# Up pieces of a tile side by side, the second piece's low products first, and down steps in groups of one or two

## The chip, the cores and the metric

The kernel runs on one core of a Trainium2 chip. The metric is the device time of one execution in microseconds (us); lower is better. Times of before are three runs: a median of 1104.94 us, from 1104.69 to 1105.36.

Five engines take part, each with its own in-order list of instructions: TensorE (PE: matrix products; PEld is its loading of the stationary operand), VectorE (DVE), ScalarE (ACT), GpSimd (POOL) and SyncE (SP). In this kernel SP and POOL issue the transfers. Engines wait for each other by semaphores.

## The reference

One layer of a transformer on 256 tokens of width 2048, in float32: two groups of eight attention heads, an output projection, and a feed-forward network (FFN) with a short causal convolution. The change is about the FFN's products, and about a helper that the second attention group uses too.

```python
def conv_ffn(h, w_up_l, conv_w_l, conv_b_l, w_down_l):
    u = h @ w_up_l                                  # (256 x 2048) @ (2048 x 11264)
    c = u.shape[-1]
    u = lax.conv_general_dilated(u, conv_w_l[:, None, :], ..., padding=[(2, 0)],
                                 feature_group_count=c) + conv_b_l
    gate, val = jnp.split(u, 2, axis=-1)
    return (jax.nn.silu(gate) * val) @ w_down_l     # (256 x 5632) @ (5632 x 2048)
```

## The kernel before

**Splits.** Products run in a rounded float32 type. To keep precision every operand is split in a high half (rounded) and a low half (the rest), and a product is made of three: high times high, high times low, low times high. For a weight tile of 128 x 2048 values (1 MB) `load` (L201) brings the raw values, ScalarE casts the high half (L208, `w_hi`) and VectorE subtracts the low half (L209, `w_lo`).

**Up pieces.** `from_features` (L250) makes a piece: 8 slices of 128 rows of the weight against the features `hT`, for two blocks of 128 output columns. The 16 high products (L257) have 512 columns, since `hT` holds its high and low halves side by side; the 16 low products (L264) have 256, with the high half of `hT` alone. In before, the high products of a piece always come first. Two pieces (kh = 0 and 1) add up to a tile of 256 features in PSUM, in one bank pair `pu`; tiles come in twos, one for the gate and one for the value. The first tile of the FFN (c0 = 0) does this in two halves of 4 slices. `feature_major` uses the same helper in the second attention group (8 tiles).

**Down steps.** The down product of a part of the FFN is done for two halves of the columns (c = 0 and 1024), each in seven products instead of eight (a scheme of Strassen's kind, with sums of activations prepared in `val_follows` and sums of weights in `down_in_seven`). Each product is a step: `in_three` (L230) with 8 high and 4 low products of 512 columns. In the order of before:

1. the split activations (pairs) of the first token half with `w11` (bank_a), loads `w11`
2. the sum T5 with `w` = `w11` + `w12` (bank_b), loads `w12`; `first_sum` (L999, VectorE) makes `w`; after the split POOL issues two accumulating transfers (L969): `w22` into `w` and `w22` into `w12`
3. pairs with `w21` (bank_c), loads `w21`
4. S2 with `w` (bank_a), then `w21` is accumulated into `w`
5. T7 with `w12` (bank_a), the third sum of weights
6. S4 with `w22` (bank_b), loads `w22`
7. pairs with `w` (bank_a)

After a step VectorE adds its bank to the output rows (`added`, L946).

**What follows an up tile.** ScalarE copies half of the tile (L847), VectorE adds it (L848, `t`) and scales (L850, `up`); ScalarE forms the three taps (L857, L864), VectorE adds them (L869); then Silu for a gate tile, or, for a value tile, the product (L884), its split (L887, L889) and, in the second half of a part, four combinations (L901 to L904). When a part's last value tile is done, its sums are cast (L911, four on ScalarE) and subtracted (L916, four on VectorE).

**The order.** The FFN's 44 blocks of 128 gate columns (and the 44 of the values) are cut into six parts, five of 8 blocks and a last one of 4; a tile is two blocks. `ORDER` and `LAST_ORDER` write out which step follows which: `u` is an up piece, `s` a down step of the part before, a digit a plain down piece of the last part. A loop over the steps records all instructions under a manual schedule, so each engine's list has their order: at step n the load of step n+6, what follows earlier tiles (`follow`, twice in each step), the split of step n+2, the first sum of step n+4, and then the products of step n. The buffers: 4 raw tiles (`wraw2`), 3 high and 3 low (`whi2`, `wlo2`); in attention there are 3, 2 and 2. A buffer is given back when its last reader is done, so a high half of step n+2 waits for the high products of step n-1.

Of the kernel before, what the change touches and what calls it, by code (L numbers as in the profile page):

```python
# [14 lines left out]
P = 128  # L15
D = 2048
S = 256
NT = S // P
KT = D // P
# [5 lines left out]
NFT = DFF // P  # L25
# [12 lines left out]
FFN_PARTS = [(f, min(f + 8, NFT)) for f in range(0, NFT, 8)]  # L38


ORDER = "uuusususususususususususususus"
LAST_ORDER = "uususususususussss0s1ss3s2"


@with_exitstack
def hybrid_layer(
# [19 lines left out]
    nc = tc.nc  # L66
# [65 lines left out]
    hT = big.tile([P, KT, 2, S], F32R, name="hT")  # L132
# [86 lines left out]
    def rows_of(w, k0, n, c0, cols):  # L219
        return w[k0 * P : (k0 + n) * P, c0 : c0 + cols].rearrange("(k p) c -> p k c", p=P)  # L220
# [17 lines left out]
    def token_major(lhs, w, k0, nk, c0, cols):  # L238

        acc = psa.tile([P, NT, 512], F32, name="acc", tag="acc")  # L240
        for k in range(0, nk, 4):
            parts = weights(rows_of(w, k0 + k, 4, c0, cols), 4, cols)
            in_three(
                [acc[:, t, :cols] for t in range(NT)], parts, 4,
                lambda i, part, t: of_half(lhs(k + i), part, t), k == 0, k + 4 == nk,
            )
            step()
        return acc

    def from_features(acc, parts, kh, n=8):  # L250

        hi, lo = parts
        for i0 in range(0, 8, n):
            for i in range(i0, i0 + n):
                k = 8 * kh + i
                for j in range(2):
                    nc.tensor.matmul(  # L257
                        acc[:, j, :], hi[:, i, j * P : (j + 1) * P],
                        hT[:, k].rearrange("p a b -> p (a b)"), start=k == 0, stop=False,
                    )  # L260
            for i in range(i0, i0 + n):
                k = 8 * kh + i
                for j in range(2):
                    nc.tensor.matmul(  # L264
                        acc[:, j, S:], lo[:, i, j * P : (j + 1) * P], hT[:, k, 0, :],
                        start=False, stop=k == KT - 1,
                    )

    def feature_major(w, c0, pool, tag):

# [14 lines left out]
    with ExitStack() as actx:  # L285
# [9 lines left out]
        def project(c0, cols):  # L295
            return token_major(lambda k: hT[:, k], wi, 0, KT, c0, cols)
# [198 lines left out]
        low = big.tile([P, 2, 16 * P], F32R, name="low", tag="x2")  # L495
# [41 lines left out]
        for j in range(3):  # L537
            acc = project(2 * WF + 344 * j, 344)
            n = 344 if j < 2 else 336
# [211 lines left out]
        for half in range(2):  # L751
# [6 lines left out]
            acc = project(B0 + 2 * WF + 512 * half, 512)  # L758
# [16 lines left out]
        for group in range(2):  # L775
# [3 lines left out]
            for c in range(4):  # L779
                acc = token_major(lambda k: oT[group * NH + k], wo, group * NH, NH, 512 * c, 512)  # L780
# [6 lines left out]
                if c == 0:  # L787
                    pg = psb.tile([P, NT], F32, name="pg", tag="t")
                    for t in range(NT):
                        nc.tensor.matmul(  # L790
                            pg[:, t : t + 1], ssq[group][:, t * P : (t + 1) * P], ones[:, 0:1],
                            start=t == 0, stop=t == NT - 1,
# [86 lines left out]
    T5, S2, S4, T7 = (0, 1), (1, 1), (1, 0), (0, 0)  # L879
# [71 lines left out]
    def down_in_seven(part, c0):  # L951


        nk = (part.f_hi - part.f_lo) // 2
        w11, w12, w21, w22 = (
            rows_of(wd, part.f_lo + nk * h, nk, c0 + i * 512, 512) for h in range(2) for i in range(2)
        )
        mem = {}

        def of_pairs(h, t):  # L960
            return lambda i, p, _: part.pairs[(nk * h + i) // 2][:, p, i % 2, t * P : (t + 1) * P]

        def of_sums(q):
            n, t = q
            return lambda i, p, _: part.sums[i // 2][:, p, n, i % 2, t * P : (t + 1) * P]

        def plus(into, src):

            nc.gpsimd.dma_start(  # L969
                mem[into][:, : nk * 512].rearrange("p (a b) -> p a b", a=nk), src, accum_op=ALU.add  # L970
            )

        def product(bank, new, lhs, weights, to, op=ALU.add, load_=None, sums=None, then=None):
            t, h = to

            def loads():
                for name, src in load_ or ():
                    mem[name] = load(src)

            def prepare():  # L980
                mem["parts", bank, to] = split(mem[weights], nk, 512)
                if then:
                    then()

            def matmuls():
                if new:
                    pool, tag = (psf, "a") if bank == "bank_a" else (psb, "t")
                    mem[bank] = pool.tile([P, 512], F32, name=bank, tag=tag)
                in_three([mem[bank]], mem["parts", bank, to], nk, lhs(), new, True, more=not new)

            new_step(
                loads, sums, prepare, matmuls,
                lambda: added(c0 + 512 * h, mem[bank], t, op),
            )

        def first_sum():
            mem["w"] = wsum.tile([P, 2048], F32, name="w_sum", tag="w_sum")
            w, x, y = (mem[m][:, : nk * 512] for m in ("w", "11", "12"))
            dve.tensor_tensor(w, x, y, op=ALU.add)  # L999

        product("bank_a", True, lambda: of_pairs(0, 0), "11", (0, 0), load_=[("11", w11)])
        yield
        product(
            "bank_b", True, lambda: of_sums(T5), "w", (1, 1), load_=[("12", w12)],
            sums=first_sum, then=lambda: (plus("w", w22), plus("12", w22)),
        )
        yield
        product("bank_c", True, lambda: of_pairs(1, 0), "21", (0, 0), load_=[("21", w21)])
        yield
        product("bank_a", False, lambda: of_sums(S2), "w", (0, 1), ALU.subtract, then=lambda: plus("w", w21))  # L1010
        yield
        product("bank_a", False, lambda: of_sums(T7), "12", (1, 1), ALU.subtract)
        yield
        product("bank_b", False, lambda: of_sums(S4), "22", (0, 1), load_=[("22", w22)])
        yield
        product("bank_a", False, lambda: of_pairs(1, 1), "w", (1, 0))
        yield

    def down_plain(part, c):

        n = (part.f_hi - part.f_lo) // 4

        ends = LAST_ORDER[-1] == str(c // 512)
        sizes = [(0, 0, 512), (1, 0, 256), (1, 256, 256)] if ends else [(t, 0, 512) for t in range(NT)]
# [41 lines left out]
            piece(kh)  # L1066
            yield

    last = None
    for f_lo, f_hi in FFN_PARTS:  # L1070
        part = Part(f_lo, f_hi)
        steps_of = {

            "u": [
                p for f in range(f_lo, f_hi, 2) for follows in (gate_follows, val_follows)
                for p in [up_pieces(part, f, follows)] * 2
            ],
            "s": [g for c in (0, 1024) for g in [down_in_seven(last, c)] * 7 if last],
        }
        if f_hi == NFT:  # L1080
            steps_of |= {str(i): [down_plain(part, 512 * i)] for i in range(4)}
        for g in ORDER if f_hi < NFT else LAST_ORDER:
            if steps_of[g]:
                next(steps_of[g].pop(0))
        assert not any(steps_of.values())
        last = part

    ctx.enter_context(
# [76 lines left out]
```

## Time and profile before

| | before |
|---|---|
| median of three runs | 1104.94 us |
| profiled execution | 1104.87 us |
| its span, first to last instruction | 1103.1 us |
| instructions in it | 14847 |
| L257, high products of up pieces | 1664 |
| L264, low products of up pieces | 1664 |
| splits into halves (L208, L209) | 226 each |
| transfers from HBM | 242.89 MB |

The profile is of one execution, on the hardware. Busy times of PE are modelled and products overlap in the pipeline, so its cadence is read from the starts of successive products in the timeline, not from their lengths. A group in the timeline has its start, its length, the engine, the line, the operation, the tiles, the shapes and how often it comes; in brackets stands how long the engine was idle before it and what ended that. In the table of stretches ("windows") each row has the stretch, then the busy time of PE, PEld, DVE, ACT and POOL with their counts, the granted clock of TensorE as a share of full speed, the busy share of the DMA engines and the GB/s. In the list of waits a row has who waited for whom, the sum in us, how often, and the longest.

### The profile page before, as it was taken

The numbers are of one execution on the slowest core, as the hardware profiler recorded it, in microseconds if no ns is written. First come the engines' busy times: TensorE is split into PE (matmuls) and PEld (weight loads), VectorE is DVE, ScalarE is ACT, GpSimd is POOL, SyncE is SP. The second block draws the span as 40 slices with busy tenths as digits, with TensorE's granted clock in tenths as the row PEclk, the third lists the DMA queues.
The fourth block names the chain that finished last, engine by engine and source line by source line (L and its number), as shares of the span: only waits on it lengthen the run. The fifth ranks groups of instructions, "written<-read, shape, count | busy, mean of one in ns | idle before, by whom it ended". The sixth has DMA issues, their size and how long they took to land. (4 is left out here: it accounts for less than half of the span.)

```text
span 1103.1 us, 14847 instructions
## 1 busy us (share of the span) xinstructions
PE 1097.9 (100%) x5872; PEld 951.4 (86%) x5872; DVE 876.2 (79%) x940; ACT 701.6 (64%) x879; POOL 44.4 (4%) x46
## 2 busy tenths in 40 slices
PE   9999999999999999999999999999999999999998
PEld 7998888888888888888888888888888888888887
DVE  5755787785775677679889988889798889889896
ACT  6543565664553567667767776767676677677753
POOL 0000000000000000000000010100000010100010
PEclk9999999999999999999999999999999999999999
DMA  8776555565555396558989597986979688987985
GB/s 290 187 230 229 189 153 160 175 217 182 184 160 187 112 318 202 188 176 208 288 225 309 191 235 263 263 268 176 318 207 308 212 219 277 247 265 196 326 210 167
DMA packets 179407, 245.96 MB, mean 223 GB/s; under 512 B 4432, under 2 KB 119018, under 8 KB 179082
## 3 DMA queue, kind: packets, MB, share of 16 engines
q1 hardware_dynamic: 162458, 209.73, 58.4%
q0 software_dynamic: 16560, 34.75, 16.6%
q8 instruction: 46, 0.75, 0.3%
q10 hardware_dynamic: 320, 0.53, 0.2%
q14 instruction: 23, 0.19, 0.0%
HBM read 242.89 MB, written 2.11 MB: 222 GB/s over the span
## 5 line engine op out<-in xcount | busy, mean ns | idle before, releaser
L209 DVE TENSOR_TENSOR w_lo<-w_raw,w_hi 128x2048 fp32r<-128x2048 f32 (+1 forms) x196 | 439.7, 2246 | 148.7 <-ACT w_hi L208 148.0
L208 ACT CAST w_hi<-w_raw 128x2048 fp32r<-128x2048 f32 (+1 forms) x196 | 367.3, 1876 | 278.6 <-PE pu L257 83.4
L257 PE MATMUL pu<-hT,w_hi 128*128 128x512 f32 x1664 | 397.1, 390 | 0.0
L257 PEld LDWEIGHTS pu<-hT,w_hi 128*128 128x128 f32 x1664 | 309.4, 188 | 62.4
L264 PEld LDWEIGHTS pu<-hT,w_lo 128*128 128x128 f32 x1664 | 213.6, 191 | 8.3
L264 PE MATMUL pu<-hT,w_lo 128*128 128x256 f32 x1664 | 216.2, 283 | 0.0
L230 PE MATMUL acc<-w_hi,hT 128*128 128x512 f32 (+1 forms) x576 | 124.9, 368 | 0.0
L230 PEld LDWEIGHTS acc<-w_hi,hT 128*128 128x128 f32 x576 | 101.2, 188 | 14.1
L209 DVE TENSOR_TENSOR w_lo<-w_sum,w_hi 128x2048 fp32r<-128x2048 f32 x30 | 68.7, 2290 | 19.8 <-ACT w_hi L208 19.8
L208 ACT CAST w_hi<-w_sum 128x2048 fp32r<-128x2048 f32 x30 | 57.3, 1909 | 42.4 <-PE pu L257 36.3
L864 ACT ACTIVATE tap<-up,ccol 128x256 f32<-128x256 f32 x176 | 74.6, 495 | 0.0
L230 PE MATMUL acc<-w_lo,hT 128*128 128x512 f32 (+1 forms) x288 | 65.0, 367 | 0.0
L230 PEld LDWEIGHTS acc<-w_lo,hT 128*128 128x128 f32 x288 | 51.5, 188 | 7.4
L969 POOL DMA_DIRECT2D w_sum<-in_w_down_dram x20 | 25.7, 1285 | 796.8 <-DVE w_lo L209 786.1
L230 PE MATMUL acc<-w_hi,oT 128*128 128x512 f32 x192 | 46.0, 392 | 0.0
L230 PEld LDWEIGHTS acc<-w_hi,oT 128*128 128x128 f32 x192 | 35.7, 188 | 7.3
L230 PE MATMUL bank_a<-w_hi,s 128*128 128x512 f32 x160 | 40.1, 393 | 0.2 <-DVE x L946 0.2
L230 PE MATMUL bank_a<-w_hi,g 128*128 128x512 f32 x160 | 40.0, 392 | 0.0
L230 PE MATMUL bank_b<-w_hi,s 128*128 128x512 f32 x160 | 40.0, 392 | 0.0
L230 PEld LDWEIGHTS bank_a<-w_hi,s 128*128 128x128 f32 x160 | 28.8, 189 | 5.8 <-issue 0.6
L230 PEld LDWEIGHTS bank_a<-w_hi,g 128*128 128x128 f32 x160 | 28.9, 189 | 5.2
L230 PEld LDWEIGHTS bank_b<-w_hi,s 128*128 128x128 f32 x160 | 28.9, 189 | 5.3
(214 smaller groups left out, 1071.7 us busy)
## 6 DMA issues: line engine op xcount, KB each, us to landing
w_raw<-in_w_up_dram SPq DMA_DIRECT2D x88, 1024.0 KB, 8.0
w_raw<-in_w_down_dram SPq DMA_DIRECT2D x44, 1024.0 KB, 6.4
w_raw<-in_w_in_dram SPq DMA_DIRECT2D x36, 1024.0 KB, 5.2
w_sum<-in_w_down_dram POOLq DMA_DIRECT2D x20, 1024.0 KB, 9.7
w_raw<-in_w_out_dram SPq DMA_DIRECT2D x16, 1024.0 KB, 5.0
w_raw<-in_w_down_dram POOLq DMA_DIRECT2D x10, 1024.0 KB, 14.7
w_raw<-in_w_in_dram SPq DMA_DIRECT2D x12, 688.0 KB, 4.0
w_raw<-in_w_in_dram SPq DMA_DIRECT2D x6, 512.0 KB, 7.0
```

The source lines that it names most:

```text
L208: act.copy(hi[:, :n], raw[:, :n])
L209: dve.tensor_tensor(lo[:, :n], raw[:, :n], f32(hi[:, :n]), op=ALU.subtract)
L230: nc.tensor.matmul(o, lhs(i, l, t), r[:, i, :], start=starts and j == 0, stop=stops and j == 3 * n - 1, skip_group_check=more,)
L257: nc.tensor.matmul(acc[:, j, :], hi[:, i, j * P : (j + 1) * P], hT[:, k].rearrange("p a b -> p (a b)"), start=k == 0, stop=False,)
L264: nc.tensor.matmul(acc[:, j, S:], lo[:, i, j * P : (j + 1) * P], hT[:, k, 0, :], start=False, stop=k == KT - 1,)
L864: act.activation(taps[w][:, j, :], u[:, j, w : w + S], AF.Copy, scale=ccol[:, w, f : f + 1])
L969: nc.gpsimd.dma_start(mem[into][:, : nk * 512].rearrange("p (a b) -> p a b", a=nk), src, accum_op=ALU.add)
```

## The change

Three edits.

1. `from_features`: the second piece of a tile (kh = 1) does its low products before its high ones. The flag that ends a group of sums moves from the last low product to the last high one. The helper's other users get the same order.
2. `ORDER` and `LAST_ORDER`: the two up pieces of a tile stand side by side, and down steps between them in groups of one or two. Since that leaves one more down step than there is room for in a part, the list of down steps is kept over the parts: the seventh product of the second half of a part is done in the next part, beside the first of the next. In the second part, where nothing is left over, the first group is one step. The last part has pieces side by side for its first tile only; after that pieces and down steps alternate.
3. In `down_in_seven` S4's step with `w22` stands ahead of T7's, the third sum's.

```diff
-ORDER = "uuusususususususususususususus"
-LAST_ORDER = "uususususususussss0s1ss3s2"
+ORDER = "uu" + "ssuu" * 3 + "suu" + "ssuu" * 3 + "s"
+LAST_ORDER = "uussusususususussss0s1ss3s2"
...
         hi, lo = parts
+
+        def high(k, i, j):
+            nc.tensor.matmul(
+                acc[:, j, :], hi[:, i, j * P : (j + 1) * P],
+                hT[:, k].rearrange("p a b -> p (a b)"), start=k == 0, stop=k == KT - 1,
+            )
+
+        def low(k, i, j):
+            nc.tensor.matmul(
+                acc[:, j, S:], lo[:, i, j * P : (j + 1) * P], hT[:, k, 0, :], start=False, stop=False,
+            )
+
         for i0 in range(0, 8, n):
-            for i in range(i0, i0 + n):
-                k = 8 * kh + i
-                for j in range(2):
-                    nc.tensor.matmul(
-                        acc[:, j, :], hi[:, i, j * P : (j + 1) * P],
-                        hT[:, k].rearrange("p a b -> p (a b)"), start=k == 0, stop=False,
-                    )
-            for i in range(i0, i0 + n):
-                k = 8 * kh + i
-                for j in range(2):
-                    nc.tensor.matmul(
-                        acc[:, j, S:], lo[:, i, j * P : (j + 1) * P], hT[:, k, 0, :],
-                        start=False, stop=k == KT - 1,
-                    )
+            for product in (low, high) if kh else (high, low):
+                for i in range(i0, i0 + n):
+                    for j in range(2):
+                        product(8 * kh + i, i, j)
...
+        product("bank_b", False, lambda: of_sums(S4), "22", (0, 1), load_=[("22", w22)])
+        yield
         product("bank_a", False, lambda: of_sums(T7), "12", (1, 1), ALU.subtract)
-        yield
-        product("bank_b", False, lambda: of_sums(S4), "22", (0, 1), load_=[("22", w22)])
         yield
         product("bank_a", False, lambda: of_pairs(1, 1), "w", (1, 0))
...
-    last = None
+    last, downs = None, []
     for f_lo, f_hi in FFN_PARTS:
         part = Part(f_lo, f_hi)
+        order = (ORDER if f_hi < NFT else LAST_ORDER).replace("ss", "ss" if downs else "s", 1)
+        downs.extend(g for c in (0, 1024) for g in [down_in_seven(last, c)] * 7 if last)
...
-            "s": [g for c in (0, 1024) for g in [down_in_seven(last, c)] * 7 if last],
+            "s": downs,
...
-        for g in ORDER if f_hi < NFT else LAST_ORDER:
+        for g in order:
             if steps_of[g]:
                 next(steps_of[g].pop(0))
-        assert not any(steps_of.values())
+        assert len(downs) == (1 if last and f_hi < NFT else 0)
+        assert not any(steps_of[g] for g in steps_of if g != "s")
```

So in parts three to five the down steps stand in groups as follows, with the two pieces of one tile between any two groups: (7, 1), (2, 3), (4, 5: `w22`), (6: T7) alone, and the same again for the second half of the columns.

## The prediction

> **What bounds the kernel now.** I read the page first, then who waits for whom, then the FFN stage in windows.
>
> ```profile
> span 1103.1 us, 14847 instructions
> PE 1097.9 (100%) x5872; PEld 951.4 (86%) x5872; DVE 876.2 (79%) x940; ACT 701.6 (64%) x879; POOL 44.4 (4%) x46
> PEclk9999999999999999999999999999999999999999
> ```
>
> ```profile
> PE idle L379 <- DVE zeros L369: 1.1, 1, 1.1
> PE acc L426 <- DVE w_hi L407: 0.6, 1, 0.6
> PE bank_a L230 <- DVE x L946: 0.2, 1, 0.2
> ...
> ACT w_hi L208 <- PE pu L257: 119.7, 61, 4.2
> ```
>
> ```profile
> 503.00:1058.00 555.00, 555.00 (x2963) 481.00 (x2962) 491.54 (x431) 391.78 (x432) 34.92 (x27) 1.00 0.88 249
> ```
>
> TensorE never rests: in the whole span it waited 1.9 us for others, and the clock stayed at full. From 503 to 1058 us, where up pieces and down steps mix, VectorE is busy for 491.5 of 555 us (89%) and the DMA engines at 0.88. So time can be won only inside TensorE's own cadence, and lost wherever VectorE falls behind, since it has 11% to spare. The last line of the waits shows the brake on working ahead: the high half of a split (ScalarE, `w_hi`) waits for TensorE to give back one of three buffers.
>
> The cadence stands in the timeline of PE (start, length, what; differences of starts count, ends overlap):
>
> ```profile
> 441.51 3.82 PE L257 MATMUL pu<-hT,w_hi 128*128 128x512 f32 x16
> 445.16 2.08 PE L264 MATMUL pu<-hT,w_lo 128*128 128x256 f32 x16
> ...
> 602.18 2.00 PE L230 MATMUL bank_b<-w_hi,s 128*128 128x512 f32 x8
> 604.02 1.07 PE L230 MATMUL bank_b<-w_lo,s 128*128 128x512 f32 x4
> 604.93 3.79 PE L257 MATMUL pu<-hT,w_hi 128*128 128x512 f32 x16
> 608.55 2.08 PE L264 MATMUL pu<-hT,w_lo 128*128 128x256 f32 x16
> 610.47 0.86 PE L230 MATMUL bank_a<-w_hi,g 128*128 128x512 f32 x3
> ```
>
> Sixteen high products take 3.62 us after a down step (604.93 to 608.55), but 3.65 after low products of 256 columns (441.51 to 445.16); eight down products after low ones take 1.84, against 1.81 at the same rate. A switch from 256 to 512 columns costs 0.03 us. An up piece is 5.54 us, a down step 2.72 without the switch.
>
> **The change, part by part.** *Switches.* Counted in the order of instructions, 108 places where a 512-column product follows a 256-column one become 68. 40 x 0.03 is 1.2 us. The 48 switches the other way that also go may have been a little cheap (the low sixteen take 1.91 or 1.92 us, so at most 0.01 each); I take **-1.0 us**, bounds -1.3 and -0.5.
>
> *The tail.* T7's product is now one s step later, behind w22's.
>
> ```profile
> 1078.17 1.98 PE L1042 MATMUL acc<-w_lo,g 128*128 128x512 f32 x8
> 1080.35 2.09 PE L230 MATMUL bank_a<-w_hi,s 128*128 128x512 f32 x8 [0.20 <-DVE x L946]
> ```
>
> Eight products from 1078.17 end their cadence at 1079.99, and T7's first product starts at 1080.35: 0.36 us in which bank_a's earlier result was still to be added. With w22's product (bank_b, added long before) between them this goes: **-0.3 us**, bounds -0.4 and 0.
>
> *The moved load.* Each w22 step brings a 1 MB load on SP, two splits, twelve products and one addition, all unchanged in number; its load moves ahead in SP's queue past two up loads, and POOL's accumulating transfers keep their order. `w12` holds one of four raw buffers until T7 is split, so longer; in the changed order `w21`'s load then waits for the low half of the step three ahead of its own.
>
> ```profile
> w_raw<-in_w_up_dram SPq DMA_DIRECT2D x88, 1024.0 KB, 8.0
> w_raw<-in_w_down_dram SPq DMA_DIRECT2D x44, 1024.0 KB, 6.4
> ```
>
> It is so issued about 4.4 us after a group's start; its own step begins 5.44 + 11.08 + 2.72 = 19.2 us after it, and its split takes 4.2 of them (below). That leaves 10 us for a landing of 6.4. I cost it at 0; without that cover it is the second rival.
>
> *Pairs of pieces, and low products first.* This is where I expect the loss. Two down steps side by side last 5.44 us, but the work that hangs on the tile just finished and on both steps is still queued on VectorE; and the second piece of the next tile now needs its **low** half at its first product, 3.6 us earlier than before. Let T be the start of a group of two down steps. The high half for the next tile's first piece needs the buffer of the piece that ended at T. From there every instruction on VectorE, in the changed order, can be priced from rows where before does the same:
>
> ```profile
> 621.39 2.29 DVE L999 TENSOR_TENSOR w_sum<-w_raw 128x2048 f32<-128x2048 f32 x1
> 623.59 0.69 DVE L889 TENSOR_TENSOR g<-gate,g 128x512 fp32r<-128x512 f32 x1
> 624.19 0.42 DVE L901 TENSOR_TENSOR gate<-gate 128x256 f32<-128x256 f32 x1
> ...
> 625.91 2.28 DVE L209 TENSOR_TENSOR w_lo<-w_raw,w_hi 128x2048 fp32r<-128x2048 f32 x1
> 628.12 0.68 DVE L848 TENSOR_TENSOR t<-pu,t 128x512 f32<-128x512 f32 x1
> 628.83 0.69 DVE L850 TENSOR_TENSOR up<-t,R 128x512 f32<-128x512 f32 x1
> 629.44 2.49 DVE L916 TENSOR_TENSOR s<-gate,s 128x512 fp32r<-128x512 f32 x4
> 631.85 2.28 DVE L209 TENSOR_TENSOR w_lo<-w_sum,w_hi 128x2048 fp32r<-128x2048 f32 x1
> 634.05 1.48 DVE L869 TENSOR_TENSOR gate<-gate,tap 128x512 f32<-128x512 f32 x2
> 635.45 0.68 DVE L946 TENSOR_TENSOR x<-x,bank_a 128x512 f32<-128x512 f32 x1
> 636.05 2.28 DVE L209 TENSOR_TENSOR w_lo<-w_raw,w_hi 128x2048 fp32r<-128x2048 f32 x1
> ```
>
> ```profile
> 622.65 1.92 ACT L208 CAST w_hi<-w_raw 128x2048 fp32r<-128x2048 f32 x1 [2.72 <-PE pu L257]
> 624.47 2.19 ACT L911 CAST s<-gate 128x512 fp32r<-128x512 f32 x4
> 626.55 0.58 ACT L847 COPY t<-pu 128x512 f32<-128x512 f32 x1
> ...
> 636.46 1.91 ACT L208 CAST w_hi<-w_raw 128x2048 fp32r<-128x2048 f32 x1 [0.26 <-PE pu L257]
> ```
>
> ```profile
> 632.63 3.79 PE L257 MATMUL pu<-hT,w_hi 128*128 128x512 f32 x16
> 636.26 2.08 PE L264 MATMUL pu<-hT,w_lo 128*128 128x256 f32 x16
> 638.17 2.00 PE L230 MATMUL bank_b<-w_hi,s 128*128 128x512 f32 x8
> ```
>
> At a part's beginning (parts three, four and five), where the group is the old part's seventh product and the next half's first: ScalarE starts the high half at T+0.20 (636.46 against 636.26) and ends it at 2.11; VectorE subtracts the low half from 2.1 to 4.3 (start to start 2.2). Then ScalarE's four casts (624.47 to 626.55, 2.08) stand ahead of its copy of the tile, which ends at 4.7. VectorE: t 0.71, up 0.61, the first sum 2.20, four s differences 2.41, one addition 0.60, and the second piece's low half 2.28: 4.7 + 8.81 = 13.5. TensorE would be there at 2.72 + 2.72 + 5.54 = 10.98. It waits **2.6 us** with the hand-over, three times: **+7.8**. In before the sum ran a step ahead of the four differences (621.39), the low half came 6.3 us ahead of its step (631.85 against 638.17), and no two down steps met. What is late next: nothing. The following low half ends at 13.5 + 2.00 (taps and an addition, 634.05 to 636.05) + 2.28 = 17.8, and the down step that it feeds reaches its low products at 13.6 + 5.54 + 1.81 = 20.9.
>
> In the last part the pieces alternate after the first group, and its sum stands before T. The work queued there ahead of T (low half, sum, g difference 0.60, four combinations 624.19 to 625.91, from about T-3.2) ends at T+3.5; then 2.2 + 0.71 + 0.61 + 2.41 + 0.60 + 2.2 + 2.00 (634.05 to 636.05) + 2.28 end at 16.5, while TensorE arrives at 2.72 + 2.72 + 5.54 + 2.75 = 13.73: **+2.8**.
>
> The same group in the middle of parts two to five has the sum but neither casts nor differences: 4.3 + 0.71 + 0.61 + 2.20 + 0.60 + 2.28 = 10.7, against 10.98. A margin of 0.2 us with the hand-over: 0 to 0.3 each, I take 0.1, **+0.4** for four. Groups without a sum have 2.4 us to spare.
>
> *Attention's eight tiles.* Here two buffers hold the splits, and a second piece's high half is given back 1.9 us later. The tightest low half of a second piece:
>
> ```profile
> 242.93 2.28 DVE L209 TENSOR_TENSOR w_lo<-w_raw,w_hi 128x2048 fp32r<-128x2048 f32 x1
> ...
> 247.53 1.64 PE L257 MATMUL pu<-hT,w_hi 128*128 128x512 f32 x6
> ```
>
> It ends 2.3 us before the piece starts; less 1.9 leaves 0.4. I take 0; if VectorE's other work comes between, +0.5 for one or two pieces.
>
> Sum: -1.0 - 0.3 + 7.8 + 2.8 + 0.4 = +9.7. The profiled execution took 1104.87 us (span 1103.1), 0.07 below the median of the three runs, so I predict **1114.6 us**.
>
> **The rivals.** *The sum is out of the way (not slower).* If VectorE gets to the first sum ahead of T (its 2.20 us then fill idle time), the chain at the parts' beginnings ends at 11.3, and TensorE waits 0.4 instead of 2.6; in the last part, 0.6. That is 1.2 + 0.6 - 1.3 = +0.5: **1105.4**. It decides from 2.2 us of the 8.81 on. For it: the 63.5 us in which VectorE rests in the window. Against it: in the changed order the sum stands behind the tile's `up`, which needs the piece that ends at T.
>
> *Transfers are late too.*
>
> ```profile
> 651.23 3.76 ACT L208 CAST w_hi<-w_raw 128x2048 fp32r<-128x2048 f32 x2 [3.60 <-DMA w_raw<-in_w_up_dram]
> ```
>
> Before already has a high half that waited 3.60 us for its load, beside an accumulating transfer. In the eight groups of fourth product and w22's, a 3.6 us delay would use up the 2.4 us and leave 1.2: +9.6, **1124**. Against it: these groups have no sum, and the transfers are as many as before.
>
> *The clock drops in the gaps.* No row here has a gap of 2.6 us in the middle of the work, so the trace cannot exclude that the granted clock falls after one. If the stalled piece then ran at half the clock, four pieces cost 5.54 more each: +22, **1137**, as an upper bound. [...] No run here shows it yet.
>
> *The switches are not what costs.* Then the first term is 0 and the time 1115.6; this lies within the forecast.
>
> **How the numbers follow.** The chain of VectorE is a sum of durations in a fixed order, so I give the forecast 0.74, with 1110 to 1119 as its own range: the stalls' terms may be off by 0.4 each, the middle groups 0 to 1.2, attention 0 to 1. The early sum 0.12, late transfers 0.09, the clock 0.02, and 0.03 for a gain that I don't see. 1108 to 1121 holds the forecast and the smaller sizes of late transfers, and leaves 2 in 10 out. This kernel's measurement can tell 0.2%, 2.2 us, from no change: slower 0.84, the same 0.12 (the early sum), faster 0.04.
>
> **What would show it.** In the changed profile: PE waits for `w_lo` of DVE at the low products of an up piece, four long ones (2 to 3 us) near the starts of parts three to six, none over 0.5 elsewhere; sixteen high products take 3.62 us in nearly all pieces; in each stall VectorE runs low half, t, up, sum, four s, addition, low half without a pause. I am wrong if PE's waits stay under 2 us in all, if the sum starts before T, or if the waits name a DMA.

## The result, and the profile after

| | before | after |
|---|---|---|
| median of five runs | 1104.94 us (1104.69 to 1105.36) | 1151.78 us (1149.12 to 1152.73) |
| ratio after / before | | 1.042, 95% interval 1.041 to 1.043 |
| profiled execution | 1104.87 us | 1149.12 us |
| mean granted clock in it | 1.000 | 0.985 |

The change costs 4.2%, where 0.9% was forecast. In the profiled execution 44.3 us are to be found. First the page of after, then its clock summed over the span, then the list of waits (who waited for whom, us in all, how often, the longest):

```profile
span 1147.3 us, 14821 instructions
PE 1114.2 (97%) x5872; PEld 964.7 (84%) x5872; DVE 877.0 (76%) x940; ACT 694.4 (61%) x879; POOL 44.4 (4%) x46
PEclk9999999999999999999998999999998999999999
```

```profile
core 0: 1147.3 us, clock 0.985
```

```profile
PE pu L261 <- DVE w_lo L209: 27.7, 9, 4.2
...
ACT w_hi L208 <- DMA w_raw<-in_w_up_dram: 61.6, 22, 7.0
ACT w_hi L208 <- DMA w_raw<-in_w_down_dram: 20.8, 9, 4.5
```

The work of VectorE and ScalarE is nearly the same (877.0 and 694.4 us, in before 876.2 and 701.6). TensorE now waits nine times for low halves, 27.7 us in all. A mean clock of 0.985 over 1147.3 us is 34 us at half clock; 30.9 us of these lie outside the waits and can cost half of that, 15.4. Waits and clock so make up 43.1 of the 44.3. But the prediction had only four of the nine waits, and the last two lines say where to look for the others: ScalarE's high half waited 61.6 us for loads of up pieces, where before had 28.2 us, and 20.8 us for loads of down steps, where before had none. Eight of these nine are the eight `w22` loads.

**The four waits that were forecast.** VectorE, then TensorE, at the beginning of part three in after (start, length, engine, line, operation, tiles; in brackets the idle time before it and what ended it):

```profile
630.55 2.29 DVE L209 TENSOR_TENSOR w_lo<-w_raw,w_hi 128x2048 fp32r<-128x2048 f32 x1 [0.81 <-ACT w_hi L208]
633.11 0.69 DVE L850 TENSOR_TENSOR t<-pu,t 128x512 f32<-128x512 f32 x1 [0.27 <-ACT t L849]
633.84 0.69 DVE L852 TENSOR_TENSOR up<-t,R 128x512 f32<-128x512 f32 x1
634.45 2.28 DVE L1001 TENSOR_TENSOR w_sum<-w_raw 128x2048 f32<-128x2048 f32 x1
636.65 2.49 DVE L918 TENSOR_TENSOR s<-gate,s 128x512 fp32r<-128x512 f32 x4
639.06 0.68 DVE L948 TENSOR_TENSOR x<-x,bank_a 128x512 f32<-128x512 f32 x1
639.66 2.28 DVE L209 TENSOR_TENSOR w_lo<-w_raw,w_hi 128x2048 fp32r<-128x2048 f32 x1
```

```profile
628.36 1.98 PE L230 MATMUL bank_a<-w_hi,g 128*128 128x512 f32 x8
...
637.43 2.07 PE L261 MATMUL pu<-hT,w_lo 128*128 128x256 f32 x16
642.00 3.21 PE L261 MATMUL pu<-hT,w_lo 128*128 128x256 f32 x16 [2.50 <-DVE w_lo L209]
645.01 4.37 PE L255 MATMUL pu<-hT,w_hi 128*128 128x512 f32 x16
```

The group starts at T = 628.36, and the second piece's low half is ready at 641.94, T+13.58; the prediction's chain had 13.5, in this order. TensorE waits 2.50 us. In the last part the end of the chain was put at T+16.5 and the wait at 2.8:

```profile
1058.76 3.47 PE L261 MATMUL pu<-hT,w_lo 128*128 128x256 f32 x16 [2.68 <-DVE w_lo L209]
```

After both waits sixteen low products, elsewhere 1.91 us from start to start, take 3.0 and 3.3: the granted clock was 0.50 from 642.73 to 646.14 us and from 1059.15 to 1062.56.

**The waits that were not forecast.** A second piece behind the group of S2's product and w22's, in the second half of part two. ScalarE, GpSimd's issues, SP's issues and TensorE:

```profile
589.56 1.92 ACT L208 CAST w_hi<-w_raw 128x2048 fp32r<-128x2048 f32 x1 [3.56 <-DMA w_raw<-in_w_down_dram]
593.87 1.91 ACT L208 CAST w_hi<-w_raw 128x2048 fp32r<-128x2048 f32 x1 [2.40 <-DMA w_raw<-in_w_up_dram]
...
602.00 1.90 ACT L208 CAST w_hi<-w_raw 128x2048 fp32r<-128x2048 f32 x1 [5.74 <-DMA w_raw<-in_w_up_dram]
```

```profile
573.40 1.27 POOL L971 DMA_DIRECT2D w_sum<-in_w_down_dram  x1 [44.97 <-DVE w_lo L209]
574.15 1.82 POOL L971 DMA_DIRECT2D w_raw<-in_w_down_dram  x1
588.43 1.27 POOL L971 DMA_DIRECT2D w_sum<-in_w_down_dram  x1 [12.46 <-DVE w_lo L209]
```

```profile
575.33 0.37 SPq L201 DMA_DIRECT2D w_raw<-in_w_down_dram  x1
579.11 19.39 SPq L201 DMA_DIRECT2D w_raw<-in_w_up_dram  x4
```

```profile
600.27 2.07 PE L261 MATMUL pu<-hT,w_lo 128*128 128x256 f32 x16
606.28 3.78 PE L261 MATMUL pu<-hT,w_lo 128*128 128x256 f32 x16 [3.94 <-DVE w_lo L209]
```

The wait of 3.94 us is put down to VectorE's `w_lo` like the others. But VectorE had nothing else to do: its low half stood behind ScalarE's cast, which had waited 5.74 us for a load. At 573 and 574 us two accumulating transfers are issued, w22's load follows at 575.33, and four up loads from 579.11 on. `w22` itself is late: ScalarE waits 3.56 us for it, until 589.56, 14.2 us after its issue. TensorE doesn't feel that, since the load was issued 18.6 us ahead of its step (593.92). Stretches of after (busy time of PE, PEld, DVE, ACT, POOL with counts, granted clock, busy share of the DMA engines, GB/s) show what meets there, and the clock behind two of the waits:

```profile
555.00:565.00 10.00, 10.00 (x46) 8.28 (x45) 7.44 (x6) 5.87 (x7) 0.00 (x0) 1.00 0.13 29
565.00:573.40 8.40, 8.40 (x54) 7.60 (x53) 8.29 (x8) 5.87 (x8) 0.00 (x1) 1.00 0.99 339
573.40:583.24 9.84, 9.84 (x45) 8.15 (x44) 8.31 (x7) 7.00 (x10) 2.57 (x2) 1.00 0.87 174
583.24:602.00 18.76, 18.76 (x106) 16.45 (x105) 13.44 (x15) 6.63 (x5) 1.27 (x1) 1.00 1.10 279
...
605.18:612.01 6.83, 5.73 (x22) 5.25 (x23) 6.61 (x6) 5.42 (x7) 0.00 (x0) 0.50 0.67 216
...
642.73:646.14 3.41, 3.41 (x16) 3.22 (x15) 3.41 (x4) 2.42 (x2) 0.00 (x0) 0.50 0.91 298
```

From 555 to 565 us the DMA engines move nearly nothing (0.13), while the next load waits for a raw buffer to be given back (13.4 us, until a low half is done). With plain loads alone they then move 339 GB/s at a share of 0.99; with the two accumulating transfers and w22's load 174 GB/s at 0.87. In the 19 us after that (1.10) the second of the two still runs until 591.2, a third is issued at 588.43, and the up loads share the engines with them. The second up load of the four, issued at 583.24, is ready at 602, after 18.7 us, and TensorE, which had 2.4 us to spare there, has used them up and 3.94 more. Full DMA engines alone are not what is new: in before they stand at 1.03 to 1.10 from 565 to 605 us without a wait of TensorE. New is which loads stand in the queue there.

### The profile page after: what moved, and what is told of

The parts are those of the page before. It is cut to its first block, busy times and chain, and to the rows that moved or that the text cites. A ratio compares the mean times of both kernels' runs of the same rounds, so it can differ in the third digit from the quotient of the medians.

```text
span 1147.3 us, 14821 instructions
## 1 busy us (share of the span) xinstructions
PE 1114.2 (97%) x5872; PEld 964.7 (84%) x5872; DVE 877.0 (76%) x940; ACT 694.4 (61%) x879; POOL 44.4 (4%) x46
## 4 chain that ended last, share of the span: by engine, by line
PE 76%; DMA 9%; DVE 8%; ACT 3%; issue 3%; ACTq 0%; DVEq 0%
PE pu L255 26%; PE acc L230 21%; PE pu L261 15%; DMA w_raw<-in_w_up_dram 9%; PE bank_a L230 5%; DVE w_lo L209 4%; ACT w_hi L208 3%; PE acc L428 2%; PE bank_b L230 1%; PE acc L1044 1%; DVE x L948 1%; DVE w_sum L1001 1%; PE bank_c L230 1%; DVE t L850 1%; DVE s L918 1%
## 5 line engine op out<-in xcount | busy, mean ns | idle before, releaser
L261 PE MATMUL pu<-hT,w_lo 128*128 128x256 f32 x1664 | 223.1, 293 | 27.8 <-DVE w_lo L209 27.7
L261 PEld LDWEIGHTS pu<-hT,w_lo 128*128 128x128 f32 x1664 | 218.2, 200 | 34.4 <-DVE w_lo L209 30.0
L859 ACT ACTIVATE val<-up,ccol 128x256 f32<-128x256 f32 x44 | 24.1, 595 | 23.9 <-DVE up L852 23.7
L859 ACT ACTIVATE gate<-up,ccol 128x256 f32<-128x256 f32 x44 | 24.0, 593 | 19.3 <-DVE s L918 11.7
```

The source lines that it names most:

```text
L261: nc.tensor.matmul(acc[:, j, S:], lo[:, i, j * P : (j + 1) * P], hT[:, k, 0, :], start=False, stop=False,)
L859: act.activation(a[:, j, :], u[:, j, 2:], AF.Identity, scale=ccol[:, 2, f : f + 1], bias=ccol[:, 3, f : f + 1],)
```

## The experiments

Fifteen kernels, each run and profiled once beside the kernel before on the same chip (1104.6 to 1105.6 us). A sixteenth, the changed kernel with the first sum ahead of the split in its own step, deadlocks and has no time. Times, and what TensorE waited for:

| run | time, us | TensorE's waits over 0.5 us in the FFN, before its first plain down product |
|---|---|---|
| edit 3 undone | 1174.1 | 8 of 3.7 to 4.8 for bank_a, 3 of 2.5 and 1 of 2.7 for w_lo |
| edit 1 undone | 1131.3 | 7 of 0.8 to 3.6 for w_hi |
| sum a step earlier | 1132.3 | 8 for w_lo, 18.4 in all |
| high first at four starts | 1161.1 | 7 for w_lo, 24.3; 3 for w_hi, 10.0; 1.2 for an addition |
| before with edit 3 alone | 1110.7 | 2 for w_hi, 1.7 in all; 1.1 for an addition |
| before with edit 1 alone | 1110.2 | 1.2 for w_lo; 2 of 0.6 and 0.7 for additions |
| after, waits filled | 1153.9 | 3 of 3.4 to 4.1 for w_lo, in new places, and 3 of up to 0.9; 1.2 for an addition |
| edit 3 undone, single step third | 1115.7 | 3 of 1.3 to 1.4 and 1 of 2.9 for w_lo |
| the same, high first at starts | 1129.2 | 4 for w_lo, 14.0 in all; 2 for w_hi, 2.0 |
| single step third, sum earlier | 1115.4 | 4 for w_lo, 6.7 in all |
| the same, high first at starts | 1127.3 | 4 for w_lo, 13.3 in all; 2 for w_hi, 1.5 |
| after, no transfer into w12 | 1119.0 | 3 of 2.5 and 1 of 2.7 for w_lo |
| the same, waits filled | 1116.3 | 1 of 0.6 for w_lo |
| single third, high first, no transfer into w12 | 1106.0 | none |
| before with gaps made | 1271.7 | as made |

### One edit undone

```diff
-        product("bank_b", False, lambda: of_sums(S4), "22", (0, 1), load_=[("22", w22)])
-        yield
         product("bank_a", False, lambda: of_sums(T7), "12", (1, 1), ALU.subtract)
         yield
+        product("bank_b", False, lambda: of_sums(S4), "22", (0, 1), load_=[("22", w22)])
+        yield
```

> The changed kernel with edit 3 undone: T7's product ahead of w22's again. Theory (the four waits of 4.1 to 4.4 us in the second halves, and 1.3 us at 814, come from w22's load and the longer hold of w12, which bunch the transfers): these five go, with their drops of the clock; the waits at the parts' starts stay (three of 2.6, one of 2.8 us), each with a stretch at half clock of 3.4 us (1.5 us lost). 1104.9 - 1.0 (switches) + 10.8 + 6 = about 1121 us. Rival (the order of the steps alone bunches them): the four waits stay and the time is within 5 us of 1149.

It took 1174.1 us, more than the changed kernel: neither theory had this. The waits for late up loads are gone (ScalarE waits 7.4 us for them, 61.6 in after), but new ones stand in their place. VectorE in that run, and TensorE:

```profile
598.07 4.49 DVE L209 TENSOR_TENSOR w_lo<-w_raw,w_hi 128x2048 fp32r<-128x2048 f32 x2 [1.83 <-ACT w_hi L208]
602.48 0.68 DVE L850 TENSOR_TENSOR t<-pu,t 128x512 f32<-128x512 f32 x1
603.20 0.69 DVE L852 TENSOR_TENSOR up<-t,R 128x512 f32<-128x512 f32 x1
603.81 0.68 DVE L948 TENSOR_TENSOR x<-x,bank_a 128x512 f32<-128x512 f32 x1
```

```profile
604.63 1.62 PE L230 MATMUL bank_a<-w_hi,s 128*128 128x512 f32 x3 [4.77 <-DVE x L948]
```

S2 and T7 use the same bank, and side by side T7 must wait until VectorE has added S2's result, which stands behind two low halves, t and up: 4.77 us. So edits 2 and 3 hang together. With edit 2 alone the bank is the limit; edit 3 takes that wait away, at the price of w22's load standing two up loads earlier. Since these waits give the transfers time, the run doesn't tell which cause the late loads have.

```diff
-            for product in (low, high) if kh else (high, low):
+            for product in (high, low):
```

(with the flag that ends the sum moved back to the low products)

> The changed kernel with edit 1 undone: high products first in both pieces, so a low half is needed 3.6 us later. Both theories: the waits for the low half at the parts' starts go. Theory (loads come late too): the high halves still come late in the group of the fourth product and w22's; a piece then starts when the cast is done, 2.3 us before the low half would be: four waits of about 1.9 us, or eight if the waits at the parts' starts had given the transfers a rest; no stretch at half clock; 1112 to 1120 us. Rival (all waits are VectorE's chain, the late loads only follow from it): no wait over 0.5 us and about 1105 us.

1131.3 us: the waits for low halves go, as both theories had it, but late loads stay, and more than forecast: three of the waits for `w_hi` exceed 2.5 us and bring the half clock as well (mean clock 0.994 over 1129.5 us).

```profile
PE pu L255 <- ACT w_hi L208: 15.2, 8, 3.6
```

### VectorE's chain alone

```diff
+            for ahead in (SUM, SUM + 1):
+                if (n + ahead < EARLY) == (ahead > SUM):
+                    at(ahead, 1)
-            at(SUM, 1)
```

> The changed kernel with the first sum recorded one step earlier (five steps ahead of its product) in parts two to five. The chain of VectorE is 2.2 us shorter at the starts of parts three to five: 2.6 us of waiting become 0.4 there, with no drop of the clock, and the 2.8 us of the last part stay. The sum also gives back w11's raw buffer earlier. If late loads need only that: no wait for them is left and the time is about 1104.9 - 1.3 + 1.2 + 2.8 + 1.5 = 1109 us. If they are a backlog that each earlier wait only let run off: one wait of 3 to 4 us for each part, in first or second halves, with its drop of the clock: 1125 to 1140 us.

1132.3 us. At the three starts 1.2 us stay instead of 0.4: the sum now runs before T, but with it the four combinations and T's low half move back. The waits of 4 us in the second halves are gone; one in each of parts three to five, in the first half, has come in their place (4.2, 4.0 and 3.1 us). This is the backlog that the second case describes.

```diff
-                from_features(cell[0], mem["parts"], kh, 8 if c0 else 4)
+                from_features(cell[0], mem["parts"], kh, 8 if c0 else 4, (part.f_lo < 16 or c0 != (part.f_lo * P + DFF)))
```

(the new argument says whether the second piece does its low products first)

> The changed kernel with high products first in one second piece of each of parts three to six alone, that of the value tile behind the part's first group, where the prediction puts the 2.6 and 2.8 us. The chain of VectorE is as long, but the low half is needed 3.6 us later. Theory: these four waits go, with their drops of the clock, and nothing else changes on VectorE; the waits for loads stay, one of 3 to 4 us in each part, perhaps in another half: 1149 - 4 x (2.7 + 1.4) = about 1133 us. Rival (the waits for loads came from the VectorE stalls): about 1104 us.

1161.1 us, a miss for both. The four waits go, but TensorE reaches the next groups 2.5 us earlier, and ten waits now stand in both halves of the parts, with 76.4 us in which ScalarE waits for up loads (61.6 in after). The stalls at the starts had given the transfers time. A wait that is removed is not saved when the next resource in line has no slack.

### Edits put into the kernel before

> The kernel before with edit 3 alone: w22's product ahead of T7's in the old order of pieces and steps. w12 is held two steps longer, as in the changed kernel. If the longer hold of w12 makes the loads late: waits for high or low halves of up pieces beside the fourth product, in sum 5 to 20 us. If the grouping of the steps does it: no wait over 0.5 us, and the 0.36 us at the tail gone: 1104.6 us.

1110.7 us against 1105.1: edit 3 costs 5.6 us by itself. ScalarE's waits for up loads in this run:

```profile
ACT w_hi L208 <- DMA w_raw<-in_w_up_dram: 68.0, 18, 6.8
```

In before these were 28.2 us, 13 times. Most of it is still covered: the waits of TensorE that the profile names make up only a part of the 5.6 us. Edit 3, which moves w22's load and holds w12 longer, is enough to make up loads late, without the groups.

> The kernel before with edit 1 alone: low products first in second pieces, in the old order of pieces and steps. Theory (a low half needed 3.6 us earlier is late where VectorE was done less than 3.6 us ahead of the piece; the trace of before has ten such pieces, by 0.6 to 3.5 us): waits of 3.0, 2.0, 1.6, 1.3, 1.0 us and less, some of them shortened since each gives VectorE time, in sum 5 to 11 us, less 0.6 for 21 fewer switches, and one or two stretches at half clock: 1109 to 1117 us. Rival (the old order had time enough): no wait over 0.5 us and 1104.3 us.

1110.2 us against 1105.6, inside the range given, but not by the waits listed: one for a low half (1.2 us) and three for additions (2.0) are there, so the other pieces had their low halves in time. What else of the 4.6 us hangs on the order of the products was not followed.

### Where the loads lose their time

```diff
-ORDER = "uu" + "ssuu" * 3 + "suu" + "ssuu" * 3 + "s"
+ORDER = "uu" + "ssuu" * 2 + "suu" + "ssuu" * 3 + "suu" + "ss"
```

(and edit 3 undone, so that the groups are (7, 1), (2, 3), (S2), (T7, w22))

> The changed kernel with edit 3 undone and the single down step in the third place of the groups instead of the fourth: (7,1), (2,3), (S2), (T7, w22). S2's addition then has two up pieces of time before T7 needs the bank, and w22's load stands behind up loads again instead of ahead of them. Theory (w22's load ahead of the up loads makes these late): no wait for a load is left; the four waits of the prediction, 3 x 2.6 + 2.8 us, stay, each with at most one or two stretches at half clock: 1104.9 - 1.0 + 10.6 + 3 to 7 = 1118 to 1122 us. Rival (the longer hold of w12, one step less here, or the grouping by itself makes them late): waits of 3 to 4 us stay beside the groups of T7 and w22, and the time is over 1130 us.

1115.7 us, nearer to before than forecast. No wait for a load reaches TensorE ahead of the plain down products, and the starts of parts three to five cost 1.3 to 1.4 us instead of 2.5: the four differences of `s` run ahead of T's low half here (at 622.7 us, the low half at 625.1), where the group before holds two steps.

```profile
PE pu L261 <- DVE w_lo L209: 7.0, 4, 2.9
```

> The same with high products first in the second piece of the value tile behind the first group of parts three to six. Theory (the chain of VectorE and the place of w22's load are the two causes): no wait over 0.5 us in the FFN but the one near the end, no drop of the clock, and what is left is the change's gain from fewer switches: 1104.9 - 1.0 + 0.1 + 0 to 0.4 = about 1104.2 us. Rival (a wait taken away brings up the next one, as in the runs before): over 1112 us.

1129.2 us; the rival holds. With 1.4 us fewer at the starts the loads are late again (longest wait 4.8 us). Two more runs tried to give w11's buffer back earlier:

> The changed kernel with edit 3 undone, the single step in the third place of the groups, and the first sum recorded one step earlier in parts two to five. With the single step third there were no waits for loads, and 1.4 us at each of three starts of parts and 2.9 us in the last. Theory (the sum's 2.2 us on VectorE's chain, and w11's raw buffer, which it holds until then, are what is left): the three waits go, no wait for a load appears, and 2.9 us with one or two half-clock stretches stay in the last part: 1115.7 - 4.2 - 0 to 1 = 1110.5 to 1111.5 us. Rival (each wait taken away lets the next loads come late, as with high products first at the starts): waits of 3 to 5 us some 30 us behind the parts' starts, and over 1120 us.

> The same with high products first in the second piece of the value tile behind the first group of parts three to six, as in the run that fell to 1129.2 us without the earlier sum. Theory (there the loads came late since the first sum gave w11's buffer back late, not because of the order of the products): no wait over 0.6 us but the one near the end, no drop of the clock: 1104.9 - 1.0 + 0.1 + 1 for the end = 1104 to 1105 us. Rival (the earlier low products' wait is what gives the transfers their rest): within 5 us of 1129.

They took 1115.4 and 1127.3 us: the earlier sum neither shortens the waits at the starts here nor takes the late loads away. The place of w22's load is a cause, but not the only one.

```diff
-            sums=first_sum, then=lambda: (plus("w", w22), plus("12", w22)),
+            sums=first_sum, then=lambda: plus("w", w22),
```

First in the changed kernel:

> The changed kernel without the accumulating transfer of w22 into w12 (ten of 30 such transfers, 15 to 17 us each): T7's product then uses w12 alone, the rest of the computation is as it was. Theory (up loads are late because the DMA engines are full for some 40 us behind the accumulating transfers, and w22's load now stands ahead of them there): the waits of 4.1 to 4.4 us in the second halves go or fall under 1 us; the four at the parts' starts stay: 1104.9 - 1.3 + 10.6 + 3 to 7 = 1117 to 1121 us. Rival (the loads are late because w12 holds a raw buffer longer, whatever the traffic): the waits of over 4 us stay, and the time is over 1140 us.

Then in the rearranged one with high products first at the starts:

> The run with edit 3 undone, the single step third and high products first at the starts of parts three to six (1129.2 us), again without the accumulating transfer of w22 into w12, so that T7's product uses w12 alone. Theory (with VectorE's waits gone, full DMA engines are the one thing left): no wait over 0.6 us in the FFN but the 1 to 1.5 us near the end, no half clock, 1104 to 1105.5 us; what the switches are worth can then be read from the pieces' cadence alone, 46 fewer by 0.03 us. Rival: waits of 2.5 to 5 us stay, and the time is over 1115 us.

1119.0 and 1106.0 us. The first is the changed kernel with ten transfers fewer; T7's product then lacks `w22`, so both runs only price the transfer. Its waits:

```profile
PE pu L261 <- DVE w_lo L209: 10.2, 4, 2.7
```

How long up loads took to land, in the changed kernel and in this run:

```profile
DMA to landing us min/median/max: 4.9/6.7/19.0
DMA to landing us min/median/max: 5.0/6.5/9.9
```

Exactly the four of the prediction are left, although w12 holds its buffer as long and w22's load has its early place, and the DMA engines rest as much from 555 to 565 us (0.14). So neither the longer hold nor that rest makes loads late by itself; the traffic of the accumulating transfers does, together with what stands beside it. Whether it is the accumulating or the 1 MB more that counts, the run doesn't separate. In the second run, rearranged as the 1129.2 us one, no wait over 0.4 us is left ahead of the plain down products (the first line is the first of these):

```profile
PE acc L1044 <- DVE g L891: 0.8, 1, 0.8
PE pu L255 <- ACT w_hi L208: 0.4, 1, 0.4
```

That run shows too what the fewer switches bring: 1106.0 against 1105.6 us of before, nothing that can be seen, though from start to start each switch from 256 to 512 columns does cost 27 ns in it. Switches the other way were 7.5 ns cheap. 37 of the first kind and 45 of the second went, worth 0.7 us. The two waits shown, 1.2 us, are not in before, which has one of 0.2 in the FFN; they took it back.

### What the clock costs

> The changed kernel with 10 to 18 products by zeros of 512 columns (0.22 us each, adding nothing) at the start of eight second pieces, where TensorE stood idle 2.5 us or more, so that about 0.5 us of each wait is left idle. Theory (44 us of loss are about 29 us of waiting and 14 us of half clock): the waits are filled, not shortened, no stretch at half clock is left but where a wait moves, and the time falls by 12 to 15 us to about 1136. Rival (the drops of the clock lie inside the waits and cost nothing): within 3 us of 1149.

1153.9 us, a miss: the filled waits shrank, three stretches at half clock were left (mean clock 0.995), but late loads came back in the first halves (3.4 to 4.1 us), as in the runs above. The kernel without late loads allows the same test:

```diff
+    FILL = {50: 10, 80: 10, 110: 10, 141: 10}
...
+                for i in range(FILL.get(index, 0)):
+                    nc.tensor.matmul(cell[0][:, i % 2, :], zero[:, :P], zero, start=False, stop=False)
                 from_features(cell[0], mem["parts"], kh, 8 if c0 else 4)
```

> The run without the accumulating transfer of w22 into w12 (1119.0 us; four waits, two of them with a stretch at half clock), with ten products by zeros of 512 columns (0.22 us each) in each of the four waits, so that 0.4 to 0.7 us of each is left idle and TensorE reaches its own work no earlier. Theory (the half clock costs half of the time that its stretches last outside the wait): 6.5 us of stretches at work go, 3.2 us of time: 1115.8 us. Rival (a half clock that follows a wait costs nothing, since VectorE is what the next piece waits for): 1119 us. The four waits alone are what the prediction forecast at 1114.6 us, with 2.6 and 2.8 us for each.

1116.3 us, 2.8 less than without the filling (3.2 forecast), and TensorE comes to its own work no earlier. Before beside this run was 0.9 us faster than beside the other, so 1.8 to 2.8 is what can be told; no stretch at half clock is left in the FFN (mean clock 1.000). Four waits of VectorE's chain alone are worth 1116.3, close to the 1114.6 of the prediction.

```diff
+    def gap(acc):
+        n = GAPS[len(gaps) % len(GAPS)]
+        gaps.append(n)
+        nc.tensor.matmul(acc, zero[:, :P], zero, start=False, stop=False)
+        while n > 0:
+            nc.gpsimd.memset(zero[:, : min(n, 512)], 0.0)
+            n -= 512
+        nc.tensor.matmul(acc, zero[:, :P], zero, start=False, stop=False)
```

> The kernel before with two products by zeros of 512 columns at the start of each second piece, and between them, in seven cases of eight, memsets on GpSimd that the second product must await: 44 places, gaps in turn of about 0, 0.9, 1.3, 1.8, 2.2, 2.6, 3.1 and 4.1 us. Theory (the clock falls after any gap of 2.65 us or more, and not after 1.3): no stretch at half clock after gaps up to 1.3 us, one of 3.4 or 6.8 us after every gap of 2.6 us and more, and between these a share that grows with the gap; each stretch of 3.4 us costs about 1.7 us. [...] Time: 1104.9 + 20 for the products + 84 for the gaps + 25 to 45 for the clock: 1235 to 1255 us.

1271.7 us; the gaps came out longer than planned (109.0 us in all, not 84). The mean clock was 0.965 over 1270.0 us, which is some 89 us at half. The length of a gap alone does not decide it. Two gaps of the same length in this run, TensorE's rows behind each:

```profile
594.33 0.39 PE L831 MATMUL pu<-zero 128*128 128x512 bf16 x1 [2.39 <-POOL zero L829]
594.37 4.02 PE L257 MATMUL pu<-hT,w_hi 128*128 128x512 f32 x16
...
755.37 0.39 PE L831 MATMUL pu<-zero 128*128 128x512 bf16 x1 [2.39 <-POOL zero L829]
755.41 5.60 PE L257 MATMUL pu<-hT,w_hi 128*128 128x512 f32 x16
```

After the first the granted clock is 1.00, after the second 0.50. In after the clock changes only at multiples of 3.413 us from its other changes; here are three stretches of that length around each gap, all six on one grid of that step:

```profile
589.47:592.88 3.41, 2.46 (x11) 1.78 (x10) 3.41 (x3) 2.39 (x2) 0.54 (x2) 1.00 0.74 252
592.88:596.30 3.42, 1.97 (x9) 1.65 (x10) 3.42 (x4) 0.14 (x1) 1.27 (x3) 1.00 0.33 76
596.30:599.71 3.41, 3.41 (x23) 3.05 (x22) 1.04 (x1) 1.24 (x1) 0.00 (x0) 1.00 0.91 321
749.90:753.31 3.41, 3.08 (x15) 2.34 (x15) 3.41 (x3) 2.19 (x3) 0.00 (x0) 1.00 0.86 291
753.31:756.73 3.42, 1.36 (x6) 1.15 (x7) 3.42 (x4) 0.75 (x1) 1.81 (x4) 1.00 0.15 23
756.73:760.14 3.41, 3.41 (x9) 2.64 (x8) 1.66 (x1) 0.00 (x0) 0.00 (x0) 0.50 0.89 312
```

An edge of the grid cuts the first gap into 0.95 and 1.45 us, and the clock stays at 1.00. Of the second, 2.06 us fall into one stretch, and the next one is at 0.50. That the place on this grid is what tells them apart is an inference from two gaps and from the stretches of after (last section).

## Why the prediction was wrong

**The step that failed** is "The moved load": "That leaves 10 us for a landing of 6.4. I cost it at 0". It asked only when w22's own load would land, and took the median of all down loads for it. Beside two accumulating transfers that load took 14.2 us, not 6.4; it came in time since it was issued 0.7 us after the group's start (574.65), not 4.4. The up loads behind it were not priced, and they are what TensorE waits for: one took 18.7 us, in a stretch where the DMA engines are full, with accumulating transfers among the rest (1.10 from 583 to 602 us). Five of the nine waits, 27.7 - 10.2 = 17.5 us, come from there. Without the transfer into w12 they vanish (1119.0 us), and the four forecast stay. "Transfers are late too" was the rival that named the place, the eight groups of the fourth product and w22's; it gave 1.2 us for each and a chance of 0.09. In fact one half of a part is hit in full (about 4 us) and the other hardly. For parts three to five the runs that took the stalls at their starts away say why: such a stall lets the transfers catch up (with high products first at the starts ScalarE waited 76.4 us for up loads, 61.6 in after). The argument against it, "the transfers are as many as before", holds for the number; their order did the harm. The idle time of the DMA engines before them (0.13) may add to it, which no run separates.

**The second step** is the clock, given 0.02. All eight waits of 2.5 us and more in after bring a stretch of 3.41 or 6.83 us at half clock. What the 27.7 us of waits leave of 44.3 is 16.6 us, and the stretches outside the waits cost up to 15.4 of these. The rival's bound (5.54 us for each of four) was too high for one wait and had too few waits. The two rivals were priced one at a time, at 1124 and 1137; here both held, and the time lay beyond either. No run stood behind the 0.02: TensorE's only wait in the FFN of before is 0.2 us. In after a wait of 2.50 us was followed by 3.41 us at half clock.

**VectorE's chain at the starts of parts** was right, in its place, order and size: 2.50 and 2.68 us against 2.6 and 2.8, the four together 10.2 us against 10.6. The middle groups had a margin of 0.2 us and were forecast at 0.1 us each; there is no wait there.

**The tail** was right: no wait for bank_a is left in after's list. A new wait of 0.8 us, at the first plain down product, was not in the prediction.

**The switches**: 27 ns for each is right, but with the 7.5 ns of the switches the other way the 40 and 48 that went are worth 0.7 us, not 1.0. No run shows that as time; in the one without long waits, new waits of 1.2 us took it back.

**"No wait over 0.5 elsewhere"** was the line that should fall, and it fell; "if the waits name a DMA" did not, though a DMA is what five of them waited for. The list of waits names only the last link.

No run was faster than before. A version with the change's order, all computation and no wait was not found; low products first only where VectorE is far enough ahead, with the old order of steps, was not tried, since its few switches are worth less than a measurement can tell.

## What to carry to other kernels

When a step is moved, price not only its own transfer but each load that now stands behind it, in the stretch of the DMA engines' time in which it will run; in before a mean share of 0.88 from 503 to 1058 us hid 40 us at 1.03 to 1.10 (565 to 605). A wait names the last link, so follow each one back through the engine that it names. And when waits of TensorE are to be costed, look at the granted clock behind each as well: in after, a wait of 2.50 us was followed by 3.41 us at half clock, and up to half of that is lost as well.

## What the runs showed of the hardware

All changes of TensorE's granted clock in after lie at multiples of 3.413 us from each other (605.18, 612.01, 642.73, 646.14 and so on). Cut on that grid from 4.43 us on, the trace shows this up to 1144 us: eight stretches at full clock held 2.13 to 3.28 us of TensorE's idle time, and each was followed by one at 0.50; the others at full clock held up to 1.17 us, and none was. Of the ten stretches at 0.50, two held 1.10 and 1.80 us of idle time and were followed by another at 0.50, and eight held up to 0.37 and were followed by full clock.

In the run with gaps, TensorE was idle for 1.87 us from 734 to 741 us, at a clock of 1.00; for 3.45 us from 628 to 642, at 0.76; and for 2.86 us from 796 to 806, at 0.66.

While two accumulating transfers ran in after, the DMA engines moved far less for their busy time: 174 GB/s at a share of 0.87 (573.40 to 583.24 us), against 339 at 0.99 with plain loads alone just before (565.00 to 573.40).
